# Seven half-size products in place of eight for three projections of the first normalised input

## The chip, the cores and the metric

The kernel runs on one core of one Trainium2 chip. The metric is the device time of one execution in microseconds (us), less is better. TensorE is PE in the profile, its weight loads PEld, VectorE is DVE, ScalarE is ACT, GpSimd is POOL, and SyncE (SP) issues the DMAs.

## What is computed

The reference is two blocks of a network on 1024 tokens of width 1024. This case is about the head of the first block:

```python
h = rmsnorm(x, g_norm[layer])
proj = h @ w_in[layer]
a_u, a_v, a_gate, q, k, v, b_gate, gate_logits = jnp.split(proj, splits, axis=-1)
y_a = chunked_spatial_gating(jax.nn.gelu(a_u), jax.nn.gelu(a_v),
                             w_s[layer], b_s[layer], g_v[layer]) * jax.nn.silu(a_gate)
y_b = dilated_attention(q, k, v) * jax.nn.silu(b_gate)
g_a, g_b = jnp.split(jax.nn.sigmoid(gate_logits), N_BRANCHES, axis=-1)
merged = g_a * (y_a @ w_proj_a[layer]) + g_b * (y_b @ w_proj_b[layer])
```

Each of `a_u`, `a_v`, `a_gate` and `b_gate` is a product of the 1024 x 1024 input `h` with 1024 columns of `w_in`. After the first block come a Mamba-2 mixer, a stick-breaking attention and two gated embeddings; they are the same in both kernels.

## The kernel before

Every large product is made in fp32r with operands split into a high and a low part: `hi` is the operand rounded by a copy on ACT (L509), `lo = x - hi` is a subtraction on POOL for weights (`Gtt`, L532) and on DVE for activations (`Vtt`, L513). One 128-row step of a product is three matmuls, hi·hi, hi·lo and lo·hi (`mm`, L547), each over 512 columns. The normalised input stays in SBUF as `act1` (tiles m44r, m60r, m76r, m92r: four quadrants of 512 input rows x 512 tokens, hi and lo).

The order of all instructions is found when the kernel is built. `Sched.run` (L273) holds generator streams with priorities; it steps the stream of the lowest number among those that its own clock calls ready, and each helper (`A`, `Vtt`, `Vstt`, `Gtt`, `dma`, `mm`) adds a modelled duration to that clock. Each engine then runs its own list in that order. Memory is an arena of 4 KB units per partition (`Arena`, L70); a region that is taken as fp32 ("f") after fp32r ("r") needs the whole block between two `CUTS` to be free.

The stages around the change, in order:

- `norm_in` (L848) normalises 8 token tiles and splits them into `act1`.
- `branch_a` (L878): `gemm_a` (L612) makes `a_v` with tokens as output rows: 2 column blocks x 8 token tiles x 8 row steps x 3 matmuls. The weights of a column block are four granules, split into four 8 KB slots; a slot is released while the last token tile runs, so the second block's splits start there. `ev` (L913) applies gelu; `scale_v` (L916) takes the mean square of each finished tile (ACT, L673, then DVE, POOL) and scales it. `prep` (L893) turns `w_s` on TensorE.
- Still in `branch_a`: a loop over 8 groups makes a 128-column block of `a_u` and one of `a_gate` by `gemm_b` (L573); `half_b` (L585) takes 512 tokens: 8 row steps x 3 matmuls. `mix` (L927) makes the chunk product on TensorE for each half (fp32, 4 calls, 8 records in the trace) and then two DVE steps and one POOL step, and stores `ya` to DRAM.
- `gates_a` (L1046) makes the 8 column blocks of `b_gate` in the same way, with tanh and one DVE step as output (`spill`, L970).
- `attention1` makes, for 8 pairs of heads, v, the last gate (`gb`), q and k, and the attention between them. Its weights come from `Weights` (L366): `loads` issues a DMA per granule, 512 KB, and `splits` makes hi and lo; from here on two slots are used (`limit(2)`, L1404).

Of the kernel before, what the change touches and what calls it, by code (L numbers as in the profile page):

```python
# [69 lines left out]
class Arena:  # L70


    CUTS = (0, 8, 16, 24, 40, 44, 60, 76, 92, 108, 140, 156, 172, 192, 200, 208, 212, 216)
# [288 lines left out]
class Granule:  # L362
    pass


class Weights:  # L366
# [17 lines left out]
    def loads(self):  # L384
        yield 1.0
        for g in self.list:
            yield self.raw
# [65 lines left out]
class Builder:  # L453
# [280 lines left out]
    def load_cols(self):  # L734
# [17 lines left out]
        def fill():  # L752
            yield 15e3
            r = self.region(176, 8)
# [17 lines left out]
    def plan(self):  # L772
# [52 lines left out]
    def main(self):  # L825
# [5 lines left out]
        yield from self.gates_a()  # L831
# [16 lines left out]
    def norm_in(self):  # L848
# [5 lines left out]
        xs, nj = self.res(140, 4, 4), self.res(192, 4, 2)  # L854
        gr = self.region(164, 4)
# [22 lines left out]
    def branch_a(self):  # L878
        self.banks("01", "23", "456", "7")
        nc, a, s = self.nc, self.a, self.s  # L880
        self.ya = self.scratch("ya", [D, S])
        self.ya_tok = [Tok() for _ in range(8)]
        vr, wr = self.region(108, 32), self.region(184, 8)
        yield (vr, wr)
        v = vr.get().rearrange("p (t d) -> p t d", t=NT)
        wr.get()
        vt = [Tok() for _ in range(NT)]
        ug, ys = self.res(140, 4, 6), self.res(164, 4, 2)
        wsT, bs = self.at(184, 4).rearrange("p (g t) -> p g t", g=8), self.at(188, 4)
        nj = self.res(192, 4, 2)  # L890
        wt = Tok()

        def prep():  # L893

            yield (ug, 20e3)
            ws = ug.get()
# [9 lines left out]
            ug.put(ws, s.now)  # L906
# [4 lines left out]
        s.spawn(1, prep())  # L911

        def ev(cb, t, ps, e):  # L913
            return self.A(v[:, t, cb * 512:(cb + 1) * 512], ps, AF.Gelu_apprx_tanh, e)

        def scale_v(t, e):  # L916
            yield (nj, e)
            j = nj.get()
            r, e = yield from self.rstd(v[:, t, :], D, j, e)
            nj.put(j, e)  # L920
            vt[t].t = self.Vts(v[:, t, :], v[:, t, :], r, None, ALU.mult, dep=e)

        yield from self.gemm_a(self.act1, self.J["av"], ev, fin=lambda t, e: s.spawn(1, scale_v(t, e)))

        left = [8]

        def mix(g, u, gt, ut_, gt_):  # L927
            yield ys
            y = ys.get()
            for h in range(2):  # L930
                yield (vt, wt, ut_[h], gt_[h], self.px)
                bank = self.px.get()
                for c in range(4):
                    e = self.mm(bank[:, c * P:(c + 1) * P], v[:, h * 4 + c, g * P:(g + 1) * P], wsT[:, g, :], True, True)
                sl = slice(h * 512, h * 512 + 512)
                e = self.Vstt(y[:, sl].rearrange("p (c t) -> p c t", c=4), bank.rearrange("p (c t) -> p c t", c=4),
                              self.col["g_v"][:, g:g + 1], bs[:, g * P:(g + 1) * P].unsqueeze(1).to_broadcast([P, 4, P]),
                              ALU.mult, ALU.add, e)
                self.px.put(bank, e)
                e = self.Vtt(y[:, sl], y[:, sl], u[:, sl], ALU.mult, e)  # L940
                e = self.Gtt(y[:, sl], y[:, sl], gt[:, sl], ALU.mult, e)
            ug.put(u, e)
            ug.put(gt, e)
            left[0] -= 1
            if not left[0]:
                vr.put(e)
                wr.put(e)
            yield e
            d = self.dma(self.ya[g * P:(g + 1) * P, :], y, e)
            ys.put(y, d)  # L950
            self.ya_tok[g].t = d

        for g in range(8):
            yield (ug,)
            u = ug.get()
            yield (ug,)
            gt = ug.get()
            ut_, gt_ = [Tok(), Tok()], [Tok(), Tok()]

            def evu(dst, toks, fn):  # L960
                def e_(cb, half, ps, e):
                    toks[half].t = self.A(dst[:, half * 512:half * 512 + 512], ps, fn, e)
                    return toks[half].t
                return e_

            s.spawn(3, mix(g, u, gt, ut_, gt_))
            yield from self.gemm_b(self.act1, self.J["au", g], evu(u, ut_, AF.Gelu_apprx_tanh))
            yield from self.gemm_b(self.act1, self.J["ag", g], evu(gt, gt_, AF.Silu))
# [76 lines left out]

    def gates_a(self):  # L1046
        self.banks("01", "23", "456", "7")

        sc = self.scratch
        self.bg, self.ga, self.gb, self.ma = sc("bg", [D, S]), sc("ga", [D, S]), sc("gb", [D, S]), sc("ma", [D, S])  # L1050
        self.bg_tok, self.ga_tok, self.gb_tok, self.ma_tok = ([Tok() for _ in range(8)] for _ in range(4))
# [1246 lines left out]
```

## Time and profile before

| what | value |
|---|---|
| median of 3 runs | 3149.79 us (3147.97 to 3158.13) |
| the profiled execution | 3151.55 us, its span from first to last instruction 3149.8 us |
| TensorE busy | 3037.4 us (96% of the span) |
| DVE, ACT, POOL busy | 1680.7, 1412.5, 1126.4 us |
| mean granted TensorE clock | 0.986 |
| `a_v`, second column block | 71.45 to 118.15 us |
| `a_u`, `a_gate`, `b_gate` and the mixing | 118.15 to 393.78 us |
| first product of the attention's pairs | 393.78 us |

A line of a timeline gives start, duration, engine, line of the program, operation, output<-inputs with shapes, how many were merged, and in brackets how long the engine had been idle and what released it. Durations are as the profiler shows them; back-to-back instructions overlap a little in it, so a pace is read from start to start. A line of the busy time by stage gives the stage, its length, busy time and count of each engine, and then the granted TensorE clock, the DMA share and GB/s.

### The profile page before, as it was taken

The numbers are of one execution on the slowest core, as the hardware profiler recorded it, in microseconds if no ns is written. First come the engines' busy times: TensorE is split into PE (matmuls) and PEld (weight loads), VectorE is DVE, ScalarE is ACT, GpSimd is POOL, SyncE is SP. The second block draws the span as 40 slices with busy tenths as digits, with TensorE's granted clock in tenths as the row PEclk, the third lists the DMA queues.
The fourth block names the chain that finished last, engine by engine and source line by source line (L and its number), as shares of the span: only waits on it lengthen the run. The fifth ranks groups of instructions, "written<-read, shape, count | busy, mean of one in ns | idle before, by whom it ended". The sixth has DMA issues, their size and how long they took to land.

```text
span 3149.8 us, 40650 instructions
## 1 busy us (share of the span) xinstructions
PE 3037.4 (96%) x15374; PEld 2539.1 (81%) x15374; DVE 1680.7 (53%) x3008; ACT 1412.5 (45%) x2511; POOL 1126.4 (36%) x783
## 2 busy tenths in 40 slices
PE   7999999999999999999999999999998999998899
PEld 6888888888888888888787777778887888786787
DVE  2111137676664322547676765553447677768652
ACT  4322146666664311434242424232457777765531
POOL 3323211111111442324454542400335576658600
PEclk9999999999999999999999999999998999998999
DMA  4122312122112854332333344460201111113531
GB/s 139 57 67 69 102 59 61 58 66 62 56 54 80 273 187 148 109 89 61 97 108 104 103 105 144 142 236 27 94 23 33 40 42 48 34 47 113 196 105 54
DMA packets 270552, 290.88 MB, mean 92 GB/s; under 512 B 14660, under 2 KB 202228, under 8 KB 270356
## 3 DMA queue, kind: packets, MB, share of 16 engines
q1 hardware_dynamic: 270356, 288.29, 29.4%
q8 instruction: 120, 1.97, 0.3%
q14 instruction: 76, 0.62, 0.1%
HBM read 216.80 MB, written 71.43 MB: 92 GB/s over the span
## 4 chain that ended last, share of the span: by engine, by line
PE 47%; DVE 6%; DMA 5%; POOL 4%; issue 3%; ACT 1%; SPq 0%; POOLq 0%; DVEq 0%; ACTq 0%
PE psum L547 43%; PE psum L558 4%; DMA m92f<-acum 2%; DVE m24f L2073 1%; DVE m44f L524 1%; POOL m172f L532 1%; DMA m172f<-acum 1%; DVE m172f L513 0%; DMA m172f<-zd 0%; POOL m8r L532 0%; DVE m92f L520 0%; DMA m44f<-yd 0%; POOL m208f L532 0%; POOL m16r L532 0%; POOL smalls L532 0%
## 5 line engine op out<-in xcount | busy, mean ns | idle before, releaser
L532 POOL TENSOR_TENSOR m16r<-m0f,m16r 128x512 fp32r<-128x512 f32 (+1 forms) x70 | 118.8, 1712 | 314.7 <-ACT m16r L509 287.0
L532 POOL TENSOR_TENSOR m172f<-m172f,m24f 128x127 f32<-128x127 f32 (+7 forms) x128 | 172.7, 1358 | 138.1 <-DVE m24f L2073 108.5
L558 PE MATMUL psum<-ident,m172f 128*128 128x128 f32 (+1 forms) x1314 | 207.8, 279 | 11.4 <-POOL m172f L532 8.3
L2073 DVE TENSOR_TENSOR_SCAN m24f<-m24f,zero 128x128 f32<-128x128 f32 (+7 forms) x128 | 211.1, 1657 | 9.0 <-ACT m24f L509 8.4
L513 DVE TENSOR_TENSOR m156r<-psum,m156r 128x512 fp32r<-128x512 f32 (+2 forms) x268 | 158.3, 596 | 90.8 <-ACT m156r L509 89.4
L509 ACT ACTIVATE m156r<-psum 128x512 fp32r<-128x512 f32 (+2 forms) x268 | 140.1, 528 | 132.4 <-PE psum L558 126.6
L509 ACT ACTIVATE m192f<-psum 64x256 f32<-64x256 f32 (+2 forms) x233 | 103.6, 446 | 208.8 <-PE psum L547 112.1
L532 POOL TENSOR_TENSOR smalls<-smalls,mhalf 128x1 f32<-128x1 f32 (+1 forms) x104 | 92.2, 887 | 283.7 <-DVE smalls L520 283.6
L558 PEld LDWEIGHTS psum<-ident,m172f 128*128 128x128 f32 (+1 forms) x1314 | 156.5, 143 | 37.4 <-POOL m172f L532 11.7
L547 PE MATMUL psum<-m108r 128*128 128x512 f32 (+3 forms) x384 | 142.6, 375 | 14.8 <-ACT m172f L509 13.8
L532 POOL TENSOR_TENSOR m8r<-m0f,m8r 128x512 fp32r<-128x512 f32 (+2 forms) x38 | 72.3, 1914 | 235.9 <-ACT m8r L509 235.9
L524 DVE SCALAR_TENSOR_TENSOR m172f<-m172f,psum 128x512 f32<-128x512 f32 x63 | 42.8, 685 | 178.8 <-ACT m172f L509 141.4
L532 POOL TENSOR_TENSOR m8r<-m208f,m8r 128x512 fp32r<-128x512 f32 (+1 forms) x50 | 85.2, 1720 | 137.2 <-ACT m8r L509 137.0
L1440 DVE CUSTOM_DVE_ANT_0 m172f<-psum,m24f 128x512 f32<-128x512 f32 (+1 forms) x192 | 103.9, 554 | 55.9 <-PE psum L547 53.1
L1448 ACT ACTIVATE m172f<-m172f,smalls 128x128 f32<-128x128 f32 (+7 forms) x128 | 99.4, 776 | 75.3 <-DVE smalls L520 74.4
L547 PE MATMUL psum<-m60r,m8r 128*128 128x512 f32 x480 | 127.6, 400 | 5.0 <-DVE m108r L524 5.0
L532 POOL TENSOR_TENSOR m24r<-m0f,m24r 128x1024 fp32r<-128x1024 f32 x33 | 82.1, 2489 | 138.5 <-ACT m24r L509 135.6
L547 PE MATMUL psum<-m60r,m16r 128*128 128x512 f32 x492 | 130.8, 399 | 0.0
L547 PE MATMUL psum<-m24r,m108r 128*128 128x512 f32 (+1 forms) x504 | 130.2, 393 | 0.0
L547 PE MATMUL psum<-m44r,m16r 128*128 128x512 f32 x492 | 130.0, 397 | 0.0
L547 PE MATMUL psum<-m200r,m108r 128*128 128x512 f32 (+2 forms) x480 | 130.0, 356 | 0.0
L547 PE MATMUL psum<-m92r,m16r 128*128 128x512 f32 x492 | 129.4, 397 | 0.0
(434 smaller groups left out, 7898.8 us busy)
## 6 DMA issues: line engine op xcount, KB each, us to landing
m0f<-in_w_in_dram SPq DMA_DIRECT2D x48, 512.0 KB, 4.0
m0f<-in_m_in_dram SPq DMA_DIRECT2D x26, 512.0 KB, 4.0
m208f<-in_w_in_dram SPq DMA_DIRECT2D x24, 512.0 KB, 3.9
m92f<-acum SPq DMA_DIRECT2D x21, 512.0 KB, 9.6
m24f<-in_alibi_dram SPq DMA_DIRECT2D x16, 512.0 KB, 3.2
m172f<-zd SPq DMA_DIRECT2D x32, 256.0 KB, 9.7
yd<-m172f SPq DMA_DIRECT2D x32, 256.0 KB, 2.3
m108f<-hd SPq DMA_DIRECT2D x16, 512.0 KB, 9.3
```

Source lines behind the costliest of these rows:

```text
L509: self.nc.scalar.activation(out, in_, func, **k)
L513: self.nc.vector.tensor_tensor(out, a, b, op=op)
L524: self.nc.vector.scalar_tensor_tensor(out, a, s, b, op0=op0, op1=op1)
L532: self.nc.gpsimd.tensor_tensor(out, a, b, op=op)
L547: self.nc.tensor.matmul(out, l, r, start=start, stop=stop)
L558: self.nc.tensor.transpose(out, in_, self.ident[:in_.shape[0], :in_.shape[0]])
L1440: nc.vector.tensor_tensor_reduce(row[:, k0:k0 + w], bank[:, :w], Tt[:, off + k0:off + k0 + w], 1.0, -3e38, op0=ALU.add, op1=ALU.max, accum ...
L1448: nc.scalar.activation(row[:, :n], row[:, :n], AF.Exp, bias=nm, accum_out=l)
L2073: nc.vector.tensor_tensor_scan(x[:, ::-1], x[:, ::-1], self.zero.to_broadcast([P, n]), 1.0, op0=ALU.mult, op1=ALU.add)
```

## The change

`a_u`, `a_gate` and `b_gate` are made in 12 "quads". A quad is a pair of 128-column blocks, A1 and A2 (for a group: `a_u` and `a_gate`; for the last four: two neighbouring blocks of `b_gate`), each halved along the input rows (A11, A12, A21, A22). Times two halves of the tokens that is eight products of 4 row steps x 3 matmuls; Winograd's form of Strassen's scheme makes them from seven, with sums of weights (S1 to S4), sums of the input (T) and sums of the results.

- `sums_x` builds the T operands once into 108 to 172 KB ("r"), in four rounds. A round needs four 2 KB places (40, 42, 208, 210) together; it is 12 DVE steps of 128x512 on SBUF operands and 4 ACT copies. It can start when the input is complete.
- `quad_weights` loads the 24 column blocks (512 KB each) into four slots, makes S1 to S4 on DVE, hi on ACT and lo on POOL, 128x512 each, into four operand slots of 4 KB.
- `quad` issues the seven products of 12 matmuls and adds their results: one ACT copy, seven DVE additions with one PSUM operand, then the outputs.
- `mix` works in place and multiplies from PSUM; `ya` is stored by halves. `u` and `gate` have two slots (40 and 208), which `scale_v` uses too, and the quads' outputs wait for all eight scaled tiles.
- Loads of the attention's first weights wait until the last quad begins (`attend`); `gates_a` falls away, the last gate `gb` stays in the pairs. The `norm_in` tiles, the `a_v` tiles and the tables move to other places.

```diff
@@ plan
-        for g in range(8):
-            J["au", g] = Job(self, w, g * P, P, "b")
-            J["ag", g] = Job(self, w, 2 * D + g * P, P, "b")
-        J["bg"] = Job(self, w, 6 * D, D, "b")
+        self.attend = Tok()
...
+            J["1v", 0].blocks[0][0].go = self.attend
@@ branch_a
+        vr = [self.region(172 + 4 * t, 4) for t in range(NT)]
...
+        big = Res([self.region(40, 4), self.region(208, 4)])
...
+        X = self.sums_x()
+        self.W.split.slots = [self.W.all[i] for i in (2, 1, 3, 0)]
...
+        self.quad_weights([q for q, *_ in quads])
...
+        self.banks("01234", "", "56", "7")
...
+        for n, (q, kind, g) in enumerate(quads):
+            if n == len(quads) - 1:
+                self.W.limit(2)
+                self.attend.t = s.now
+            yield from self.quad(q, X, out_u(g) if kind == "u" else out_g(g))
+        self.r2.give(s.now)
+    def sums_x(self):
...
+        tmp = [self.region(o, 2) for o in (40, 42, 208, 210)]
+        def build():
+            yield (act.tt[0], act.tt[1], self.r2)
+            self.r2.take()
+            for k in range(4):
+                yield tmp
+                f = {}
+                for (i, j), r in zip(B, tmp):
+                    q = B[i, j]()
+                    f[i, j] = r.get()
+                    yield s.FV
+                    e = self.Vtt(f[i, j], q[:, 0, k, :].bitcast(F32), q[:, 1, k, :].bitcast(F32), ALU.add)
+                yield s.FV
+                t1 = self.Vtt(f[0, 0], f[0, 1], f[0, 0], ALU.subtract, e)
+                t3 = self.Vtt(f[0, 1], f[1, 1], f[0, 1], ALU.subtract, e)
+                yield s.FV
+                t2 = self.Vtt(f[1, 1], f[1, 1], f[0, 0], ALU.subtract, t1)
+                t4 = self.Vtt(f[1, 0], f[1, 0], f[1, 1], ALU.subtract, t2)
+                for T_, x, e in zip(T, ((0, 0), (1, 1), (0, 1), (1, 0)), (t1, t2, t3, t4)):
+                    q = T_()
+                    yield (e, s.FA)
+                    e = self.A(q[:, 0, k, :], f[x], AF.Copy, e)
+                    yield (e, s.FV)
+                    e = self.Vtt(q[:, 1, k, :], f[x], q[:, 0, k, :].bitcast(F32), ALU.subtract, e)
+                for r in tmp:
+                    r.give(e)
+            done.t = e
+        s.spawn(2, build())
+        return [(B[0, 0], None), (B[1, 0], None), (T[1], done), (T[2], done), (T[0], done), (T[3], done), (B[1, 1], None)]
+    def quad(self, q, X, out):
...
+        s.spawn(0.5, sums())
+        for o, (x, tok), d in zip(q.ops, X, done):
+            yield (o.ready, tok, self.pg)
+            d.ap = self.pg.get()
+            x = x()
+            for k in range(4):
+                self.mm(d.ap, o.hi[:, k, :], x[:, 0, k, :], k == 0, False)
+                self.mm(d.ap, o.hi[:, k, :], x[:, 1, k, :], False, False)
+                e = self.mm(d.ap, o.lo[:, k, :], x[:, 0, k, :], False, k == 3)
```

The order of a quad's weight operands is `("A11", "A12", "S2", "S3", "S1", "A22", "S4")`: the first two products use the plain input, the third is the first that waits for the sums of the input (`done`).

## Rows read from the trace of the kernel before

**Rows 1.** The page, busy time, share of the span and instructions of each engine.
```profile
PE 3037.4 (96%) x15374; PEld 2539.1 (81%) x15374; DVE 1680.7 (53%) x3008; ACT 1412.5 (45%) x2511; POOL 1126.4 (36%) x783
```
**Rows 2.** Busy time by stage: the replaced products, and the last column block ahead.
```profile
118.15:393.78 275.63, 275.63 (x1281) 230.51 (x1280) 39.23 (x50) 72.02 (x90) 83.55 (x44) 1.00 0.26 82
71.45:118.15 46.70, 44.42 (x193) 35.79 (x192) 5.60 (x13) 16.57 (x26) 13.04 (x12) 1.00 0.16 45
```
**Rows 3.** Timeline of PE: two neighbouring runs of twelve matmuls of the replaced products.
```profile
120.87 2.88 PE L547 MATMUL psum<-m76r,m8r 128*128 128x512 f32 x12
123.59 2.88 PE L547 MATMUL psum<-m60r,m8r 128*128 128x512 f32 x12
```
**Rows 4.** Timeline of PE: one half of the mixing, and the product after it.
```profile
135.84 1.05 PE L547 MATMUL psum<-m172f,m108f 128*128 128x128 f32 x8
136.64 1.62 PE L547 MATMUL psum<-m60r,m16r 128*128 128x512 f32 x6
```
**Rows 5.** Timeline at the second column block of a_v: splits on POOL, PE behind.
```profile
73.75 2.38 POOL L532 TENSOR_TENSOR m24r<-m0f,m24r 128x1024 fp32r<-128x1024 f32 x1
76.38 2.37 POOL L532 TENSOR_TENSOR m24r<-m0f,m24r 128x1024 fp32r<-128x1024 f32 x1 [0.25 <-ACT m24r L509]
78.81 1.43 PE L547 MATMUL psum<-m24r,m76r 128*128 128x512 f32 x5 [0.97 <-POOL m24r L532]
```
**Rows 6.** Groups and timeline of DVE: 128x512 steps, alone and back to back.
```profile
L513 DVE TENSOR_TENSOR m156f<-m156f,m140f 128x512 f32<-128x512 f32 x14 | 9.7, 692 | 1.5
...
1464.62 0.69 DVE L513 TENSOR_TENSOR m172f<-psum,m92f 128x512 f32<-128x512 f32 x1 [1.67 <-PE psum L558]
1465.23 0.68 DVE L513 TENSOR_TENSOR m172f<-psum,m192f 128x512 f32<-128x512 f32 x1
```
**Rows 7.** Timeline in the Mamba stage: DVE steps on SBUF beside POOL, then alone.
```profile
1431.34 3.39 POOL L532 TENSOR_TENSOR m92f<-m92f,m192f 128x1024 f32<-128x1024 f32 x1
1432.84 7.62 DVE L524 SCALAR_TENSOR_TENSOR m44f<-m60f,m192f,m44f 128x1023 f32<-128x1023 f32 x3 [0.38 <-ACT m44f L509]
...
1443.72 1.28 DVE L524 SCALAR_TENSOR_TENSOR m44f<-m92f,m192f,m44f 128x1023 f32<-128x1023 f32 x1 [0.85 <-ACT m44f L509]
```
**Rows 8.** Timeline: the mean square of one finished a_v tile, ACT to POOL.
```profile
80.90 1.06 ACT L673 ACTIVATE m192f<-m108f 128x1024 f32<-128x1024 f32 x1
82.32 0.55 POOL L532 TENSOR_TENSOR smalls<-smalls,mhalf 128x1 f32<-128x1 f32 x1 [3.56 <-DVE smalls L520]
```
**Rows 9.** Groups and timeline of POOL: steps of 128x512, gating and weight split.
```profile
L532 POOL TENSOR_TENSOR m156f<-m156f 128x512 f32<-128x512 f32 x10 | 12.9, 1288 | 52.4 <-DVE m156f L513 30.8 <-issue 21.7
...
406.31 2.53 POOL L532 TENSOR_TENSOR m8r<-m208f,m8r 128x512 fp32r<-128x512 f32 x2 [19.20 <-ACT m8r L509]
```
**Rows 10.** Timeline: a weight split on POOL queued behind a gating step.
```profile
141.51 1.05 ACT L509 ACTIVATE m16r<-m0f 128x1024 fp32r<-128x1024 f32 x1
144.97 1.29 POOL L532 TENSOR_TENSOR m156f<-m156f,m140f 128x512 f32<-128x512 f32 x1 [5.05 <-DVE m156f L513]
146.22 2.40 POOL L532 TENSOR_TENSOR m16r<-m0f,m16r 128x1024 fp32r<-128x1024 f32 x1
```
**Rows 11.** Timeline of PE at a stall, and the stage right behind it.
```profile
1829.96 0.49 PE L547 MATMUL psum<-m76f,m60f 128*128 128x128 f32 x2 [2.70 <-DVE m172f L513]
1831.44 2.76 PE L547 MATMUL psum<-m8r,m140r 128*128 128x512 f32 x6
1834.01 1.59 PE L547 MATMUL psum<-m200r,m108r 128*128 128x512 f32 x6
1830.00:1834.00 4.00, 4.00 (x12) 3.18 (x13) 1.18 (x3) 0.45 (x2) 1.28 (x1) 0.58 0.65 122
```
**Rows 12.** Weights of the attention's pairs: DMA issues (page), then one split on ACT.
```profile
m0f<-in_w_in_dram SPq DMA_DIRECT2D x48, 512.0 KB, 4.0
...
405.18 1.06 ACT L509 ACTIVATE m8r<-m208f 128x1024 fp32r<-128x1024 f32 x1 [3.29 <-issue]
```

More of the change, by code (lines that the diff above doesn't have):

```diff
@@ L362, with __init__ @@
 class Granule:
-    pass
+    go = None
+class Quad:
+    ORDER = ("A11", "A12", "S2", "S3", "S1", "A22", "S4")
+    def __init__(self, *srcs):
+        self.srcs = srcs
+        self.raw = [None, None]
+        self.loaded = [Tok(), Tok()]
+        self.part, self.tok = {}, {n: Tok() for n in self.ORDER + ("A21",)}
+        self.ops = [Granule() for _ in self.ORDER]
+        for o in self.ops:
+            o.ready = Tok()
+        self.left, self.seen = [3, 2], set()
 class Weights:
@@ L386, in loads @@
         for g in self.list:
-            yield self.raw
+            yield (self.raw, g.go)
             g.slot = self.raw.get()
@@ L753, in fill @@
             yield 15e3
-            r = self.region(176, 8)
+            r = self.region(140, 8)
             yield r
@@ L905, in prep @@
                 self.px.put(bank, t)
-            ug.put(ws, s.now)
+            r.give(s.now)
             nc.gpsimd.affine_select(wsT, wsT, pattern=[[0, 8], [1, P]], compare_op=ALU.is_ge, fill=0.0, base=0,
@@ L918, in scale_v @@
[L918 to L923, printed above, removed]
+            yield (big, e)
+            j = big.get()
+            r, e = yield from self.rstd(v[t], D, j, e)
+            big.put(j, e)
+            vt[t].t = self.Vts(v[t], v[t], r, None, ALU.mult, dep=e)
@@ L925, in branch_a, with mix @@
+        quads = []
+        w = a["w_in"][0]
+        for g in range(8):
+            quads.append((Quad((w, g * P), (w, 2 * D + g * P)), "u", g))
+        for g in range(0, 8, 2):
+            quads.append((Quad((w, 6 * D + g * P), (w, 6 * D + g * P + P)), "b", g))
+        self.quad_weights([q for q, *_ in quads])
+        yield from self.gemm_a(self.act1, self.J["av"], ev, fin=lambda t, e: s.spawn(1, scale_v(t, e)), begin=begin)
+        self.banks("01234", "", "56", "7")
         left = [8]
-        def mix(g, u, gt, ut_, gt_):
-            yield ys
-            y = ys.get()
+        def mix(g, o):
@@ L930, in mix @@
             for h in range(2):
-                yield (vt, wt, ut_[h], gt_[h], self.px)
+                sl = slice(h * 512, h * 512 + 512)
+                yield (vt, wt, o[0, h], o[1, h], self.px)
+                u, gt = o["ap"]
                 bank = self.px.get()
                 for c in range(4):
[L934 to L938, printed above, removed]
@@ L949, in mix @@
[L949 to L968, printed above, removed]
+                for r in vr + [wr, br]:
+                    r.give(e)
@@ new lines, in out_u, with out @@
+        def out_u(g):
+            o = {(i, j): Tok() for i in range(2) for j in range(2)}
+            o["ap"] = [None, None]
+            s.spawn(3, mix(g, o))
+            def out(i, j, ps, e):
+                if o["ap"][i] is None:
+                    yield (vt, big)
+                    o["ap"][i] = big.get()
+                yield (e, s.FA)
+                t = self.A(o["ap"][i][:, j * 512:j * 512 + 512], ps, (AF.Gelu_apprx_tanh, AF.Silu)[i], e)
+                o[i, j].t = t
+                return t
+            return out
@@ new lines, in branch_a, with out_g, out @@
+        ev, each = self.spill(self.res(172, 2, 4), "silu2", self.bg, self.bg_tok)
+        def out_g(g):
+            def out(i, j, ps, e):
+                yield from each(g + i, j)
+                yield (e, s.FA)
+                return ev(g + i, j, ps, e)
+            return out
+        for n, (q, kind, g) in enumerate(quads):
[3 more added lines that the diff above has]
+            yield from self.quad(q, X, out_u(g) if kind == "u" else out_g(g))
@@ L1044, in load_act @@
             act.tt[kh] = [done[kh * 4:kh * 4 + 4]] * NT
[L1046 to L1051, printed above, removed]
-        ev, each = self.spill(self.res(172, 2, 4), "silu2", self.bg, self.bg_tok)
-        yield from self.gemm_b(self.act1, self.J["bg"], ev, each=each)
     def merge(self):
```

155 lines of the change are left out of this document (132 added, 23 removed).

## The prediction

> **What bounds the kernel now.** I read the page first: TensorE is busy for 96% of the span [rows 1], no other engine for much more than half. An average says nothing of one stage, so next the busy time by stage: from 118.15 to 393.78, where `a_u`, `a_gate`, `b_gate` and the mixing are made, TensorE is busy for 275.63 of 275.63 us at granted clock 1.00, that is 2.4 GHz, with DVE at 39, ACT at 72 and POOL at 84 us [rows 2]. So the stage lasts as long as its matmuls. The timeline gives their pace: twelve start 2.72 us after the twelve before, 0.2267 us each [rows 3]. A half of the mixing holds TensorE for 0.80 us, start to start [rows 4]. Check: 1152 x 0.2267 + 16 x 0.80 = 273.9 us, within 1% of the stage. A matmul taken away here shortens the kernel by its whole pace, provided that the three other engines, which get more work, keep up. That is what the rest is about.
>
> **Products removed.** Before: 24 blocks x 2 halves x 24 = 1152 matmuls. After: 12 quads x 7 x 12 = 1008. 144 x 0.2267 = **-32.6 us**. The pattern hi, hi, lo over 512 columns is the same, so I keep the pace.
>
> The Trainium skill has another price (TensorE: Matmul & The Clock Gate, Back-to-back issue gap): about 131 ns per matmul of 512 columns in a sustained stream. By it the 144 would be worth 18.9 us and the sum below would end at 3138. This case's trace differs, at 226.7 ns, and the measurement decides.
>
> **Sums of the input, before the quads.** `sums_x` is 4 rounds of 12 DVE steps of 128x512; one takes 0.69 us, back to back they start every 0.605 us [rows 6], so 7.3 us a round; the ACT copies lie beside. The question is when the last round ends against the third product, the first that needs it. Where DVE steps with two SBUF tensors run beside POOL they take turns: three steps of 1.28 us took 7.62, and the POOL step between took 3.39 in place of 2.4 [rows 7, 10]. I count such steps of DVE and POOL in series.
>
> Start: place 208 holds raw weights until the POOL split ahead of the one at 73.75 is done, so 73.8. Two splits are still to come there, to 78.8, and TensorE waits for the last [rows 5]. One DVE step gets between them, which delays that split and TensorE by **+0.4**; the other eleven follow, so round 0 ends at about 85.9. Then `scale_v`, of lower number and so first, takes 40 and 208 for the tiles that wait. From ACT's start to POOL's end that is 2.0 us for one tile [rows 8], about 2.4 with the handover, and 1.25 more for each further one on ACT. A tile is done every 24 x 0.2267 = 5.4 us from about 80 on. So: one tile, round 1 from 88.3 to 95.6; two tiles, round 2 from 99.3 to 106.6; three tiles, round 3 from 111.4. Round 3 meets the first quad: its weight sums S1 to S3 (3 DVE steps) and four POOL halves of 1.27 us [rows 9], as the slots come free while the last `a_v` tile runs. In series 15 x 0.605 + 4 x 1.27 = 14.2 us, with one scaling step and handovers about 127.0. The third product could start at 118.15 + 0.4 + 2 x 2.72 = 124.0. **+3.0 us**, between 0 and about 9 (another tile or two served ahead of round 3, and the next POOL halves). The one stall of this length that I hold up, 2.70 us, was followed by a granted clock of 0.58, so partly at 1.2 GHz, and six matmuls took 2.57 us in place of 1.36; with the shorter work ahead of them that is **+1.7**, or 0 if the stall stays short [rows 11].
>
> The Trainium skill speaks of this step too (SBUF — State Buffer, SBUF: two separate sides): a DVE step with two SBUF inputs and a GpSimd step hold one port pair in turn, the loser blocked for the whole instruction. The trace agrees, with 3.39 beside 2.39. Without it round 3 would be over before 124.0 and the sum would be 3118, the first rival below.
>
> **Feeding the quads.** A quad takes TensorE 84 x 0.2267 = 19.0 us, and 20.6 with two halves of mixing. POOL: seven halves and two gating steps of 1.27 to 1.29 us [rows 9] = 11.5 us. A gating step also blocks POOL's queue while it waits for mixing and DVE: a split whose ACT half was over at 142.6 began at 146.2, behind a gating step that had begun at 144.97 [rows 10]; that is 2.4 us before the step itself, say 2.8, twice a quad, 5.6 us. Four weight sums on DVE in turn with POOL add 4 x 0.6. In all 19.5 of 20.6 us: close, but four operand slots let POOL run ahead and the four `b_gate` quads have no mixing. DVE has some 15 steps, 10 us; ACT 12 steps, each shorter than the 1.06 us of a 1024-wide one [rows 12]. Results lie in five banks; the longest held waits for a sum four products on, and `u` and `gate` places come free before the next quad's output asks. The order was fixed with durations that know no turns, so here and there TensorE, in order, meets mixing whose DVE input comes late. Below, this costs nothing, as the stage now; above, 16 halves x 1.27 = 20 us. I take **+2.0**, near the lower end, since the sums of results have a PSUM operand and back-to-back steps of that kind keep their pace [rows 6].
>
> **The seam to attention.** v's weights are issued only as the last quad begins: 4.0 us to land [rows 12], ACT 1.06, POOL 2.5 [rows 9], while TensorE has 19 us of quad. The gate's slot shares its block with the sums of the last quad and comes free about 1 us after it; ready 5 us after, behind v's 48 x 0.2267 = 10.9 us. Nothing, covered by quad and v; without the cover 4.0 + 1.06 + 2.5 = 7.6 us and the clock. The stores of `ya` by halves, SP's 24 loads and the moved places of `norm_in` I cost at nothing beside that; for the head and for the changed order of everything after I leave 4 us to either side.
>
> **Sum.** -32.6 + 0.4 + 3.0 + 1.7 + 2.0 = -25.5. It is made against the profiled execution, span 3149.8 and 3151.55 with what lies around; the median of the runs, 3149.79, is 1.8 lower, and the shift is applied to it: **3124.3 us**.
>
> **Rivals.**
> - *The sums are in time.* If fewer tiles are served ahead of round 3, there is no stall and no clock loss, and feeding costs nothing: -32.6 + 0.4, 3117.6. For it: two rounds lie in a stretch in which POOL does almost nothing; against: the turns of [rows 7]. Chance 0.25.
> - *POOL feeds too slowly.* If each of the nine POOL steps of a group's quad waits behind one DVE step of 0.6, POOL needs 9 x 1.87 + 5.6 = 22.4 us against 20.6, 1.8 x 8 quads = 14.4 in place of 2.0: 3136.7. Against it: only four DVE steps per quad have two SBUF operands. Chance 0.12.
> - *The attention starts late.* If v's weights land too late, 7.6 + 1.7 more: 3133.6. Against it: 19 us of cover. Chance 0.08.
> - *Both of these.* 3146.0, no change. Chance 0.06.
> - *Slower.* POOL sets the quad, at the wait that the Mamba stage shows, 1.0 us a step [rows 7]: 9 x 2.27 + 5.6 = 26.0, 5.4 x 8 = 43.5 on top of the seam: 3149.8 - 32.6 + 5.1 + 43.5 = 3165.8. It decides from the point where POOL's step takes (20.6 + 27.5/8 - 5.6)/9 = 2.05 us: then all is eaten. Against it: the DVE steps that block here are half as long. Chance 0.04.
>
> **How the numbers follow.** My forecast has the remaining 0.45, 3118 to 3131 by its own bounds. The range runs from 3114 (first rival less the 4 us) to 3138 (slow feeding); it leaves out no change, slower and some tails, under 0.2. A measurement can tell about 0.3%, 9.4 us, from no change. Faster than that: 0.45 + 0.25 + 0.12 + 0.08 = 0.90; within: 0.06; slower: 0.04.
>
> **What would show it.** Right: twelve matmuls per 2.72 us in the quads, first quad at about 118.5, one wait of TensorE for a DVE step of `sums_x` ahead of the third product, first product of attention at about 368. Wrong: the wait is missing (first rival); TensorE waits for POOL inside the group quads, and POOL's 128x512 steps there take well over 1.3 us; TensorE waits for POOL after the last quad; or the stages behind take other times than before.

## The result, and the profile after

The changed kernel took 3120.6 us (median of 4 runs, 3117.3 to 3122.8), the kernel before 3150.3 beside it: 29.7 us less, a quotient of 0.9906. The ratio on record is 0.9894, with a 95% interval of 0.9881 to 0.9908, in which that quotient lies too. A second measurement on another chip gave 0.9892 (0.9875 to 0.9909), 3124.8 against 3159.9, which is 35.1 us less. The changed kernel is faster, by about 1%; the predicted 3124.3 is 3.7 us too slow, and the time lies within the predicted range. The profiled execution had a span of 3117.9 us, 31.9 less than before.

Busy time by stage of the changed kernel: the head, the second column block of `a_v`, the quads, the rest. The columns are the window, its length, the busy time of PE, PE's weight loads, DVE, ACT and POOL with instruction counts, the granted clock, the DMA share and GB/s.

```profile
0.00:72.25 72.25, 58.00 (x266) 46.56 (x267) 24.07 (x38) 31.04 (x48) 20.56 (x25) 1.00 0.37 132
72.25:119.23 46.98, 44.74 (x194) 35.73 (x192) 39.88 (x58) 23.04 (x41) 12.40 (x10) 1.00 0.12 34
119.23:362.21 242.98, 242.98 (x1137) 203.55 (x1136) 138.20 (x182) 104.80 (x161) 132.05 (x103) 1.00 0.28 88
362.21:3117.90 2755.69, 2663.03 (x13637) 2226.48 (x13635) 1620.63 (x2911) 1293.20 (x2350) 1013.23 (x709) 0.98 0.30 94
```

Against [rows 2] the quads' stage fell from 275.63 to 242.98 us, by 32.65, and TensorE is still busy for all of it at clock 1.00. The work went to the others: DVE from 39 to 138 us, POOL from 84 to 132, ACT from 72 to 105. Before the quads there are +0.80 us (head) and +0.28 us (the column block, 46.70 to 46.98), behind them -0.33. The seam, where the forecast had its stall, on PE's timeline:

```profile
119.23 2.88 PE L563 MATMUL psum<-m44r,m24r 128*128 128x512 f32 x12
121.95 2.88 PE L563 MATMUL psum<-m76r,m24r 128*128 128x512 f32 x12
124.67 2.88 PE L563 MATMUL psum<-m108r,m24r 128*128 128x512 f32 x12
127.39 2.88 PE L563 MATMUL psum<-m140r,m24r 128*128 128x512 f32 x12
...
```

The third product (m108r, the first that reads sums of the input) starts 2.72 us after the second, at the pace of [rows 3]. There is no wait here, and none of PE in the whole stage.

Where the sums were at that time, on the timeline of DVE and, in the last row, POOL (start, time, engine, line, operation, in brackets the idle time before it):

```profile
45.96 0.68 DVE L529 TENSOR_TENSOR m40f<-m44r 128x512 f32<-128x512 f32 x1
...
74.35 2.85 DVE L529 TENSOR_TENSOR m208f<-m76r 128x512 f32<-128x512 f32 x1 [27.11 <-POOL m16r L548]
77.12 2.85 DVE L529 TENSOR_TENSOR m208f<-m92r 128x512 f32<-128x512 f32 x1
...
85.08 0.69 DVE L529 TENSOR_TENSOR m40f<-m44r 128x512 f32<-128x512 f32 x1
...
96.35 0.68 DVE L529 TENSOR_TENSOR m40f<-m44r 128x512 f32<-128x512 f32 x1
...
109.09 0.68 DVE L529 TENSOR_TENSOR m40f<-m44r 128x512 f32<-128x512 f32 x1
...
116.08 0.68 DVE L529 TENSOR_TENSOR m156r<-m208f,m156r 128x512 fp32r<-128x512 f32 x1
116.71 1.76 DVE L529 TENSOR_TENSOR m16f<-m0f 128x512 f32<-128x512 f32 x1
116.48 3.15 POOL L548 TENSOR_TENSOR m24r<-m0f,m24r 128x512 fp32r<-128x512 f32 x2 [8.09 <-ACT m24r L525]
```

The rounds begin at 45.96, 85.08, 96.35 and 109.09, and the last ends at 116.77. The first weight sum (116.71) and the first POOL halves (116.48) come only as it ends, and its last DVE step (116.08) still takes 0.68 us: the fourth round takes turns with nothing, and it is over 7.9 us ahead of the third product.

### The profile page after: what moved, and what is told of

Read it like the earlier page. It is cut to its first block, busy times and chain, and to the rows that moved or that the text cites. A ratio compares the mean times of both kernels' runs of the same rounds, so it can differ in the third digit from the quotient of the medians.

```text
span 3117.9 us, 40886 instructions
## 1 busy us (share of the span) xinstructions
PE 3008.7 (96%) x15230; PEld 2512.3 (81%) x15230; DVE 1822.8 (58%) x3188; ACT 1452.1 (47%) x2600; POOL 1178.2 (38%) x845
## 4 chain that ended last, share of the span: by engine, by line
PE 74%; DVE 8%; DMA 5%; POOL 4%; issue 4%; ACT 2%; SPq 0%; POOLq 0%; ACTq 0%; DVEq 0%
PE psum L563 68%; PE psum L574 6%; DMA m92f<-acum 3%; DVE m24f L2277 2%; DVE m44f L540 1%; POOL m172f L548 1%; DMA m172f<-acum 1%; DVE m92f L536 1%; DVE m172f L529 1%; DVE m60f L540 1%; DVE m172f L534 0%; POOL m16r L548 0%; DMA m172f<-zd 0%; POOL smalls L548 0%; DVE m76f L540 0%
## 5 line engine op out<-in xcount | busy, mean ns | idle before, releaser
L548 POOL TENSOR_TENSOR m8r<-m0f,m8r 128x512 fp32r<-128x512 f32 (+1 forms) x68 | 108.0, 1605 | 321.0 <-ACT m8r L525 293.3
L574 PE MATMUL psum<-ident,m172f 128*128 128x128 f32 x1312 | 205.3, 278 | 14.2 <-POOL m172f L548 7.8
L574 PEld LDWEIGHTS psum<-ident,m172f 128*128 128x128 f32 x1312 | 155.8, 142 | 42.0 <-POOL m172f L548 10.8
L563 PE MATMUL psum<-m108r,m24r 128*128 128x512 f32 x576 | 141.9, 395 | 0.0
L548 POOL TENSOR_TENSOR m24r<-m0f,m24r 128x1024 fp32r<-128x1024 f32 (+1 forms) x43 | 87.3, 2031 | 140.6 <-ACT m24r L525 140.0
L534 DVE TENSOR_SCALAR m172f<-m172f,smalls 128x512 f32<-128x512 f32 (+7 forms) x165 | 120.3, 729 | 28.5 <-POOL smalls L548 23.9
L525 ACT ACTIVATE m24f<-psum,rq 128x512 f32<-128x512 f32 (+1 forms) x192 | 112.6, 587 | 40.9 <-DVE psum L529 31.3
L563 PEld LDWEIGHTS psum<-m108r,m24r 128*128 128x128 f32 x576 | 108.3, 190 | 22.0
L525 ACT ACTIVATE m40f<-psum 128x512 f32<-128x512 f32 (+1 forms) x123 | 69.3, 565 | 114.8 <-PE psum L563 76.7
L548 POOL TENSOR_TENSOR m16r<-m208f,m16r 128x512 fp32r<-128x512 f32 (+1 forms) x48 | 78.6, 1656 | 101.4 <-ACT m16r L525 101.1
```

The costliest lines, as they stand in the source:

```text
L525: self.nc.scalar.activation(out, in_, func, **k)
L534: self.nc.vector.tensor_scalar(out, a, s1, None, op0=op0)
L548: self.nc.gpsimd.tensor_tensor(out, a, b, op=op)
L563: self.nc.tensor.matmul(out, l, r, start=start, stop=stop)
L574: self.nc.tensor.transpose(out, in_, self.ident[:in_.shape[0], :in_.shape[0]])
```

## The experiments

Each experiment ran beside the kernel before, which took 3159 to 3161 us on the three chips used, so ratios are compared. The changed kernel ran again on one of these chips (a0_after, 0.9892); against it the others are set by their ratios.

| kernel | median us | ratio to the kernel before (interval) |
|---|---|---|
| e1_eighth, last product twice | 3149.5 | 0.9970 (0.9960 to 0.9980) |
| f1_pinned, the same, old order | 3160.4 | 1.0003 (0.9993 to 1.0013) |
| e2_late, fourth round of sums late | 3134.5 | 0.9921 (0.9902 to 0.9940) |
| e3_pool3, 3 halves twice | 3127.5 | 0.9886 (0.9858 to 0.9914) |
| f3_pool7, 7 halves twice | 3176.6 | 1.0062 (1.0041 to 1.0082) |
| e8_attend, attention's loads late | 3135.0 | 0.9919 (0.9902 to 0.9935) |
| a0_after, the changed kernel | 3124.8 | 0.9892 (0.9875 to 0.9909) |
| f2_plan, planned 12 matmuls longer | 3114.7 | 0.9858 (0.9842 to 0.9874) |
| f8_plan18, planned 18 longer | 3119.9 | 0.9872 (0.9850 to 0.9894) |
| g1_before, before, planned longer | 3148.4 | 0.9966 (0.9955 to 0.9976) |
| e9_ga4, two more quads | 3220.7 | 1.0191 (1.0173 to 1.0209) |
| f5_limit4, four split slots | 3144.5 | 0.9956 (0.9938 to 0.9974) |

### Is TensorE still what paces the quads?

e1_eighth issues the last product of each quad twice:

```diff
                 e = self.mm(d.ap, o.lo[:, k, :], x[:, 0, k, :], False, k == 3)
+            if o is q.ops[-1]:
+                for k in range(4):
+                    self.mm(d.ap, o.hi[:, k, :], x[:, 0, k, :], k == 0, False)
+                    self.mm(d.ap, o.hi[:, k, :], x[:, 1, k, :], False, False)
+                    e = self.mm(d.ap, o.lo[:, k, :], x[:, 0, k, :], False, k == 3)
```

> The changed kernel, with the last of the seven products of each quad issued twice: 12 matmuls more on TensorE in each of 12 quads, 144 in all, nothing more to load, to add or to split (the second issue begins the sum anew, so the result is that of one). It gives TensorE back the work that the change took away and leaves the change's steps on the other engines as they are. Theory A, the quads are paced by TensorE alone and all the change's feeding lies beside it: +144 x 0.2267 = +32.6 us against the changed kernel, about 3153, so within 5 us of the kernel before (3150) and the first quad's products still 2.72 us apart. Rival B, part of the quads' time is set by the feeding (GpSimd's halves, VectorE's sums), as the prediction's +2.0 and +3.0 us assumed: TensorE's added work falls partly into that time, and the kernel gains clearly less, +26 to +29 us.

f1_pinned issues the same matmuls through `nc.tensor.matmul`, so that the planner doesn't count them and no order changes.

> The kernel with the last product of each quad issued twice once more, but the planner is not told of the second issue: every engine's order, the stages after the quads included, is now that of the changed kernel, where the first such kernel came out 4.9 us shorter behind the quads. Theory A, the quads are paced by TensorE and the difference behind them came with the plan: +32.65 us (144 x 0.2267) in the quads and within 3 us of that in the whole, so +30 to +35 us against the changed kernel beside it. Rival B, the time behind the quads varies by executions and not by plans: the quads again +32.65, but the whole between +25 and +45.

Windows of e1_eighth, then of f1_pinned: the first product of a quad to the first of the attention, and the rest.

```profile
119.40:395.20 275.80, 275.80 (x1283) 230.65 (x1282) 138.27 (x182) 104.84 (x161) 131.71 (x103) 1.00 0.25 78
395.20:3146.00 2750.80, 2657.80 (x13637) 2224.17 (x13635) 1614.48 (x2911) 1295.20 (x2350) 1023.56 (x709) 0.99 0.30 94
```

```profile
119.40:395.20 275.80, 275.80 (x1283) 230.65 (x1282) 138.29 (x183) 104.86 (x161) 132.13 (x103) 1.00 0.25 78
394.90:3157.90 2763.00, 2667.68 (x13637) 2231.05 (x13635) 1622.28 (x2911) 1293.97 (x2350) 1014.24 (x709) 0.98 0.30 93
```

From start to start the stage takes 275.63 us in both (119.53 to 395.16, and 119.26 to 394.89), 32.65 more than in the changed kernel, at the same work of DVE, ACT and POOL. All of TensorE's work counts, so theory A holds in the stage, and no part of it is paced by feeding. The whole tells it less well: e1_eighth lies 24.6 us above the changed kernel (0.0078 of 3160); f1_pinned lies 35.6 above it by the medians on one chip, just past the 35 of its theory A. Equal work, some 10 us apart by the ratios: 2750.80 and 2763.00 us behind the quads. e1_eighth by its median alone would have spoken for the rival. What differs is the order that the planner gives to the later stages, since it reckons in e1_eighth that they begin 32.6 us later.

### The plan of the later stages

f2_plan adds nothing to the chip's work but moves the planner's clock; f8_plan18 does it with `range(18)`, g1_before 144 times behind the quads' stage of the kernel before.

```diff
                 e = self.mm(d.ap, o.lo[:, k, :], x[:, 0, k, :], False, k == 3)
+            if o is q.ops[-1]:
+                for k in range(12):
+                    e = self.s.pe(226.35)
```

> The changed kernel itself, again, to stand on the same chip beside the three that follow: 3120.6 us in its first four runs (3117 to 3123) where the kernel before had 3150.3. By theory A, whatever the chip, its ratio to the kernel before is the same within 0.003: 0.986 to 0.992. Rival: the first ratio owed something to that chip, and it comes out above 0.993 or below 0.985.

> The changed kernel with nothing added on the chip, but the planner counts 12 matmuls more per quad (as if the last product were issued twice): the steps of the quads are the same work, and everything behind them is planned 32.6 us later, which shuffles the order of the later stages as in the first kernel with the doubled product. Theory A, the plan of the later stages alone is worth some us either way: the quads as in the changed kernel (first attention product at 362 us, within 1 us), and behind them -2 to -7 us as that kernel had (-4.9), 3113 to 3119 where the changed kernel has 3120.6. Rival B, that difference was the execution's: within 2 us of the changed kernel beside it. Rival C, the looser plan feeds the quads later and costs there.

> The changed kernel with nothing added on the chip, the planner counting 18 matmuls more per quad (12 in the earlier one, which came out 10 us faster than the changed kernel beside it). Theory A, the plan of the later stages is a draw: a third plan of the same work lands anywhere within 10 us of the changed kernel, quads unchanged (first attention product at 361.5 to 362.5 us), and the difference arises behind 900 us. Rival B, a planner that reckons the quads longer is better for a reason: as the earlier one, -8 to -12 us.

> The kernel before, its planner reckoning everything behind the quads 32.6 us later (144 matmuls that are not issued); nothing on the chip is added or left out. It asks whether the kernel before has the same draw in its later stages, and so how much of the measured 29.7 us between the two kernels is plan and how much the change. Theory A: its quads as before (first attention product at 393.8 us within 1 us), the whole within 10 us of the kernel before, and unequal to it by more than 2 us. Rival B: the kernel before doesn't move, within 2 us.

a0_after repeats the first ratio (0.9892 and 0.9894). f2_plan is 10.1 us faster than it on the same chip, 3.1 us more than I allowed for; f8_plan18 lies between the two (its interval reaches both); g1_before is 12.3 us faster than the kernel before, 2.3 more than allowed. The quads don't move: 242.99 us from start to start in the first three, 275.63 us in g1_before as in the kernel before. Windows of a0_after, then of f2_plan, cut where they have done nearly the same number of matmuls:

```profile
118.57:361.55 242.98, 242.98 (x1137) 203.48 (x1137) 138.17 (x182) 104.86 (x161) 131.67 (x103) 1.00 0.28 88
361.55:1305.00 943.45, 940.74 (x4926) 800.49 (x4926) 501.78 (x1239) 457.33 (x859) 219.51 (x140) 1.00 0.32 103
1305.00:1410.00 105.00, 93.04 (x511) 81.91 (x510) 48.27 (x82) 33.69 (x54) 29.38 (x15) 0.93 0.27 73
1410.00:3121.80 1711.80, 1630.70 (x8205) 1345.46 (x8203) 1073.27 (x1591) 803.40 (x1439) 765.26 (x554) 0.98 0.29 90
```

```profile
118.56:361.54 242.98, 242.98 (x1137) 203.48 (x1137) 138.17 (x182) 104.86 (x161) 131.65 (x103) 1.00 0.28 88
361.54:1305.00 943.46, 941.54 (x4933) 801.33 (x4933) 501.04 (x1240) 457.18 (x859) 218.85 (x140) 1.00 0.32 103
1305.00:1401.00 96.00, 88.99 (x500) 78.51 (x500) 50.08 (x80) 32.98 (x53) 31.11 (x15) 0.96 0.31 79
1401.00:3112.90 1711.90, 1632.96 (x8207) 1349.24 (x8206) 1063.96 (x1592) 804.39 (x1439) 771.38 (x555) 0.98 0.29 90
```

In these two executions all of the 9 us lies between 1305 and 1410. The waits of PE in that stretch, of a0_after and of f2_plan (engine, tile, line, the releaser, total, times, longest):

```profile
PE psum L563 <- issue: 7.1, 1, 7.1
PE psum L563 <- DVE m76f L540: 4.8, 1, 4.8
```

```profile
PE psum L563 <- issue: 5.8, 1, 5.8
PE psum L563 <- DVE m76f L540: 1.2, 1, 1.2
```

The two waits are 4.9 us shorter, and the mean clock is 0.96 in place of 0.93, so less of it ran at 1.2 GHz. Other kernels, too, speak for the plan and not the execution. By the traces, f2_plan gives DVE, ACT and POOL the same order of steps as e1_eighth, and f1_pinned gives them that of the changed kernel. Behind the quads the first two take 2751.3 and 2750.8 us; the three profiles of the other order take 2755.7, 2760.2 and 2763.0 us, so executions of one order differ as well. Where g1_before gains isn't shown: the one profile of the kernel before is from the first chip, and the two take 2756.0 and 2755.2 us behind the quads. Rival B of f8_plan18, that the longer reckoning is better for a reason, isn't excluded; two plans that land at -10 and -6 us, within their intervals, don't settle it. That the plan is worth about 10 us in either kernel is shown by the runs of one chip each. f2_plan is the fastest kernel here, 0.9858 of the kernel before. It does the same work as the changed kernel, and its gain over it is one of order.

### The sums of the input, late

```diff
-        X = self.sums_x()
+        X = self.sums_x(vt)
...
-                yield tmp
+                yield (tmp, vt[6]) if k == 3 else tmp
```

> The changed kernel, with the fourth round of sums of the input held until the gated tile 6 is scaled, so that it falls at 118 to 127 us, among the first quad's own weight sums and halves, where the prediction had put it, and not at 109 to 117, where the trace of the changed kernel has it. Nothing is added, left out or repeated. Theory A, the sums were simply early, and the prediction's price of being late was right: the third product (124.67 us in the changed kernel) waits for the last of the sums, 127 to 130 us, which is 2 to 6 us on TensorE, and the following stretch runs at 1.2 GHz for a while, +1.7 us; together +3 to +8 us, 3124 to 3128. Rival B, the third product does not need them that early (VectorE works off the round faster than the 7.6 us of the rounds before it, or the order of the products lets others go first): 0 to +1 us, and no wait at that product. Rival C, the wait comes but the clock stays at 2.4 GHz: the wait alone, and no stretch with a granted clock under 0.9.

The round came later than I had meant, from 128.69 us and not 118. Timeline of e2_late: PE, and of DVE the round's first step and the one that makes the low part which the third product reads:

```profile
123.77 2.20 PE L563 MATMUL psum<-m108r,m24r 128*128 128x512 f32 x9
134.01 0.79 PE L563 MATMUL psum<-m108r,m24r 128*128 128x512 f32 x1 [8.04 <-ACT m108r L525]
135.22 1.22 PE L563 MATMUL psum<-m108r,m24r 128*128 128x512 f32 x2 [0.41 <-DVE m108r L529]
136.24 4.45 PE L563 MATMUL psum<-m140r,m24r 128*128 128x512 f32 x12
140.53 2.91 PE L563 MATMUL psum<-m108r,m24r 128*128 128x512 f32 x12
...
128.69 0.68 DVE L529 TENSOR_TENSOR m40f<-m44r 128x512 f32<-128x512 f32 x1
134.48 0.68 DVE L529 TENSOR_TENSOR m108r<-m208f,m108r 128x512 fp32r<-128x512 f32 x1
```

Theory A in kind, though past its 3 to 8 us: TensorE waits 8.45 us at this product, and the stage from the first quad to the attention takes 254.33 us (118.33 to 372.66) in place of 242.99, 11.34 more; the whole, by the ratio, 9.2. What is left beside the wait, 2.89 us, is the clock (the twelve matmuls from 136.24 took 4.29 us to the next start, not 2.72). The first row also shows what the prediction missed: nine of the twelve matmuls of the third product run without the fourth round, which is wanted 9 x 0.2267 = 2.0 us after the product's start.

### GpSimd's feeding

```diff
             e = self.Gtt(R(lo), q.part[n], hi, ALU.subtract, e)
+            if n in ("A12", "S3", "A22"):
+                e = self.Gtt(R(lo), q.part[n], hi, ALU.subtract, e)
```

> The changed kernel, with three of the halves that GpSimd makes for a quad's combined weights made twice (the same values again): three more steps of some 1.3 us on GpSimd per quad, 3.9 us, and nothing more on any other engine. Theory A, by busy time alone: GpSimd has 132.05 us of work in the 242.98 us of the quads, 11.0 of 20.2 us each; with 3.9 more it is 14.9 of 20.2, and nothing changes, within 2 us of 3120.6. Theory B, by the account of the prediction, which adds the time that GpSimd's queue stands behind a wait (2 x 2.8 us) and waits for turns (4 x 0.6 us) to its work: 19.5 + 3.9 = 23.4 us for a quad of 20.2, so 3.2 us too slow in each of 12, less the lead of the first one or two: +20 to +37 us, 3141 to 3158. In between (+5 to +15 us) would say that only part of the blocked time is real.

f3_pool7 issues all seven halves a second time, through `nc.gpsimd.tensor_tensor`.

> The changed kernel with all seven halves that GpSimd makes for a quad made twice (the same values), unknown to the planner, so that every order is that of the changed kernel: seven more steps of 1.30 to 1.36 us per quad, 9.3 us. GpSimd's work rises from 11.0 to 20.3 us for a quad of 20.2 us. With three such steps (14.9 of 20.2) the first attention product had not moved. Theory A, only busy time counts: 0 to +3 us in the quads. Theory B, the time that GpSimd's queue stands behind waits (2 x 2.8 us a quad in the prediction's account) is spent only as long as there is slack, and adds once there is none: 23 to 26 us for a quad, +30 to +65 us in the quads, less the lead of the first ones, with waits of TensorE for GpSimd's halves in most quads.

The quads' stage in e3_pool3, then in f3_pool7 with PE's waits for POOL in it:

```profile
119.20:362.10 242.90, 242.90 (x1138) 203.40 (x1137) 152.29 (x182) 104.41 (x161) 187.60 (x139) 1.00 0.28 88
```

```profile
119.20:417.00 297.80, 261.84 (x1137) 207.72 (x1136) 148.49 (x182) 102.42 (x161) 244.09 (x187) 0.97 0.23 72
```

```profile
PE psum L563 <- POOL m24r L1121: 30.6, 21, 3.3
```

With 36 more steps POOL is busy for 187.60 of 242.90 us, 15.6 per quad, and the stage is not a tenth of a microsecond longer (242.99 from start to start). With 84 more it takes 298.03 us from start to start (118.94 to 416.97), 24.8 per quad. TensorE waits 21 times for POOL, 30.6 us, and runs in part at the lower clock: it is busy for 261.84 us with the same matmuls. That is theory A for the first and theory B for the second. The point from which POOL sets the pace lies between 15.6 and 20.3 us of work per quad (11.0 + 9.3); the change has 11.0. One difference isn't separated: e3_pool3's planner counts the added steps and moves some 25 of 278 DVE steps up to the end of the quads (POOL's own order stays but for one step), while f3_pool7 keeps the changed kernel's order. Why POOL's waits didn't count, by the waits of POOL and ACT in the quads' stage of the changed kernel, then two of POOL in e3_pool3:

```profile
POOL m24r L548 <- ACT m24r L525: 51.4, 44, 2.0
POOL m208f L548 <- DVE m208f L529: 25.1, 8, 3.6
POOL m40f L548 <- DVE m40f L529: 25.1, 8, 3.6
ACT m24r L525 <- PE psum L563: 116.4, 64, 3.1
```

```profile
POOL m208f L548 <- DVE m208f L529: 1.0, 1, 1.0
POOL m40f L548 <- DVE m40f L529: 1.0, 1, 1.0
```

POOL waits for ACT, and ACT for TensorE to free an operand slot. The queue stands behind waits because it is ahead. When it isn't, they shrink. The waits ahead of the 16 gating steps (m208f, m40f) are 50.2 us in the changed kernel and 2.0 in e3_pool3, where the added work fills that time. In f3_pool7 POOL waits for ACT's halves 6.8 us, not 51.4; 36.7 us ahead of gating steps remain there, and then they count.

### The attention's loads without cover

```diff
             if n == len(quads) - 1:
                 self.W.limit(2)
-                self.attend.t = s.now
             yield from self.quad(q, X, out_u(g) if kind == "u" else out_g(g))
+        self.attend.t = s.now
```

> The changed kernel, with the loads of the first attention's weights let go only after the last quad's loop, and not at its beginning; nothing is left out or repeated. It prices the prediction's rival that the attention starts late. Theory A: the cover that these loads have is needed, and without it TensorE stands after the last quad (362 us) for the load and the splitting of the first weights, up to 7.6 us, with up to 1.7 us more for the clock after it: +5 to +9 us, 3126 to 3130. Rival B: other loads or products that can go ahead cover it: 0 to +2 us.

Timeline of PE in e8_attend at the end of the last quad:

```profile
359.53 2.88 PE L563 MATMUL psum<-m92r,m24r 128*128 128x512 f32 x12
371.72 5.66 PE L563 MATMUL psum<-m44r,m8r 128*128 128x512 f32 x12 [9.31 <-ACT m8r L525]
377.22 2.92 PE L563 MATMUL psum<-m76r,m8r 128*128 128x512 f32 x12
```

Theory A, somewhat dearer: 9.31 us of waiting and 5.50 - 2.72 = 2.78 us for twelve matmuls at 1.2 GHz, 12.1 in all, where I had put 9.3. By the ratio it is +8.5 us. In the changed kernel the first attention product (362.21) follows without a gap.

### Two more quads

e9_ga4 makes four of the last gate's eight blocks in two further pairs; the merge stage then holds four split weights, not five.

```diff
-        J["ga"] = Job(self, w, 7 * D, D, "b")
+        J["ga"] = Job(self, w, 7 * D + 4 * P, D - 4 * P, "b")
...
+        for g in range(0, 4, 2):
+            quads.append((Quad((w, 7 * D + g * P), (w, 7 * D + g * P + P)), "a", g))
```

> One step further on the change's own way: the four lowest blocks of the last gate are made in two more pairs of the first attention's stage, each by seven products, instead of singly in the last stage. By the sum of the prediction this takes away 2 x 12 matmuls x 0.2267 = 5.4 us of TensorE, with 14 more weight steps of GpSimd and as many sums laid beside quads that were found with room; the order of the later stages is planned anew. Theory A: -5.4 us, and the plan's few us either way: -10 to 0 us against the changed kernel, 3111 to 3121. Rival: the attention now starts behind two more quads and the last stage has less to lay under its own waits, so that the gain is lost: 0 to +10 us.

f5_limit4 is the changed kernel with only the second part, `self.taken(self.r2, 4)` for 5.

> The changed kernel with one thing from the one with 14 quads that cost +96 us: the merge stage may hold four split weights in place of five. The last gate's eight blocks all stay in the merge. Theory A, what cost there was the missing products: half of the last gate's blocks no longer covered the loading of the merge's second input, and TensorE stood (the two 20-us stretches from 1020 had 8.60 and 11.17 us of work at 1.2 GHz). Then this one is within 10 us of the changed kernel. Rival B, the four slots cost it: +50 us or more, with the same idle stretches.

Both theories missed the first by far: +96 us. Two windows of e9_ga4 at the end of the first attention, with PE's longest waits from 1000 to 1110, then f5_limit4's first 60 us there:

```profile
1000.00:1030.00 30.00, 18.16 (x81) 13.91 (x80) 8.60 (x20) 9.56 (x19) 7.06 (x3) 0.68 0.39 130
1030.00:1060.00 30.00, 12.29 (x31) 7.04 (x31) 12.15 (x17) 10.95 (x20) 7.01 (x3) 0.50 0.58 185
```

```profile
PE psum L563 <- DVE m172f L540: 10.7, 3, 7.6
PE psum L574 <- DVE m156r L529: 10.0, 2, 7.1
PE psum L563 <- ACT m108r L525: 5.7, 3, 2.5
```

```profile
1000.00:1060.00 60.00, 60.00 (x266) 49.67 (x266) 23.00 (x28) 19.56 (x32) 26.08 (x11) 1.00 0.87 280
```

In the changed kernel the last gate's products lie beside the end of the attention and the splitting of the merge's second input. With four blocks fewer TensorE stands, falls to 1.2 GHz, and loses some 60 us here against the changed kernel, compared at equal numbers of matmuls done (7.4 us behind at the 5000th, 67.2 at the 5500th). With the four slots alone it is busy throughout, so the slots aren't the cause here; the two more quads, the missing products and the plan that follows from them are left, and the missing cover is the reading that fits where it stands.

The slots, with the plan that they bring, cost about 20 us (0.9956 against 0.9892), more than theory A's 10, and later: TensorE waits for POOL's splits of weights three times, 9.70, 11.13 and 10.39 us. The longest, on PE's timeline of f5_limit4:

```profile
1727.92 4.51 PE L563 MATMUL psum<-m108r,m16r 128*128 128x512 f32 x10 [11.13 <-POOL m16r L548]
```

e9_ga4 has the same three waits (9.87, 10.61 and 10.74 us), and the changed kernel none above 3.5 us between 1400 and 2000. So the rest of the 96 is in the main this loss, which the two kernels share. By the first part alone, these products were worth more as cover than the 5.4 us that two seventh products save.

## Why the prediction was right, and where it was not

**The products** were sized right: 144 x 0.2267 = 32.65 us, measured three times, removed in the change and put back in e1_eighth and f1_pinned. The Trainium skill's figure (TensorE: Matmul & The Clock Gate, Back-to-back issue gap), 131 ns per matmul, would make that 18.9 us; no run here shows it.

**The DVE step among the splits**, +0.4: the column block took +0.28, and +0.45 in a0_after, the same program. There were two such DVE steps, of 2.85 us each, beside the splits (the round's first two had run at 45.96, which the prediction didn't foresee), and it was mostly they that waited: the splits took 2.40 and 2.49 us, 2.38 and 2.37 before, and PE's waits for POOL in the block came to 2.2 us, 2.3 before. In a0_after the last split took 2.86 and the waits came to 2.7. So the size is about right, but that the +0.28 is the price of these steps isn't shown. That the first quad came at 119.23 and not 118.5 is the head; a0_after has it at 118.62 and its head is 0.02 us longer than before, so the +0.80 is the execution's.

**The stall at the third product, +3.0, did not come.** The step that failed is the sentence "Round 3 meets the first quad". The start was nearly right (111.4 against 109.09: the prediction served a tile between the first two rounds, and none was). But the fourth round then ran alone, in 7.68 us, and not in series with three weight sums and four POOL halves, which came as it ended. That I let POOL's halves in ahead rested on the slots coming free during the last `a_v` tile; the first began at 116.48. And the deadline was 2.0 us too early, as e2_late shows: with the third product's sums ready two DVE steps ahead of the round's end, 127.0 - 2 x 0.605 = 125.8, against 124.0 + 2.0 = 126.0, even the predicted order would have cost next to nothing. That is an estimate from these rows; no run has that order. **The +1.7 for the clock** fell with it. The mechanism is real where the wait is: 8.45 us of waiting brought 2.89 of clock in e2_late, 9.31 brought 2.78 in e8_attend.

**The feeding, +2.0, was nothing.** The failed term is "In all 19.5 of 20.6 us", which added 5.6 us of blocked queue and 2.4 us of turns to 11.5 us of work. The blocked time was sized about right, 50.2 us at 16 gating steps, 3.1 each where I had put 2.8. But blocked time that comes from being ahead isn't load: TensorE waits nowhere in the stage, and e3_pool3, 23.4 us by that account, left the stage at 242.99 us. The turns are real, though they too were hidden: DVE's 182 instructions took 152.29 us there and 138.20 in the changed kernel. By the Trainium skill (SBUF — State Buffer, SBUF: two separate sides) a DVE step with two SBUF inputs and a GpSimd step shut each other out; the rows agree, with 2.85 and 1.76 beside POOL and 0.69 alone. What was wrong was only to charge TensorE for it. The two rivals on POOL charged the same 5.6 us of blocked queue and fell with it.

**The seam to attention** went as predicted: no wait, and e8_attend shows that the cover is needed, at 12.1 in place of 9.3 us.

**The stages behind**: the prediction left 4 us to either side, which was too little. Plans of the same work lie 10.1 us (a0_after and f2_plan), some 10 (e1_eighth and f1_pinned, by their ratios) and 12.3 us (before and g1_before) apart. In the first profile the two happened to be alike, 2756.02 and 2755.69 us, so the draw didn't show.

**The sum.** In the stages the first rival came true (no stall, feeding free, -32.2): the profile has -32.65 + 0.28 + 0.80 - 0.33 = -31.9. The forecast's -25.5 was 6.4 short: 4.7 for the seam's stall and clock and 2.0 for the feeding, less 0.35 by which the stages before and behind took longer than forecast. By the medians of the first chip, -29.7, it looks nearer than its reasons were, and that is luck: by those of the second, -35.1, it is 9.6 short.

## What to carry to other kernels

An engine that feeds the bottleneck through a few slots spends its spare time in waits, so count its work per period against the period, with room to spare (here 15.6 us of 20.2 cost nothing, and 20.3 cost 4.6 a quad), and charge blocked time only when the waits that it stands behind don't end at the bottleneck. Before a late operand is priced, find the first matmul that reads it, not the first of its product. In a kernel whose order is made by a planner an edit can redraw the order of everything behind it: here that was worth up to 12 us, so compare stages in the trace, or hold the plan fixed, before a difference of whole times is put down to the edit; and products that look like mere load may be the cover for a later stage's loads.

## What was not expected of the hardware

The quads' stage repeats to 0.01 us over executions and chips (242.98 once, 242.99 in a0_after, f2_plan, f8_plan18 and e3_pool3), while the kernel before took 3150.3 on one chip and 3159 to 3161 on the others, and one program's part behind the quads 2755.7 and 2760.2 us. Where TensorE never waits, here, nothing scatters; the parts that scatter are those with waits, where the clock falls as well. After 8 to 9 us of waiting the price of the clock was 2.8 to 2.9 us, about 1.1 more than the 1.7 that was derived from a wait of 2.70 us; from 140.53 us (e2_late) and 377.22 us (e8_attend) on the pace was near 2.72 us for twelve matmuls again.
